# Tying nine kinds of instructions to written order in a two-layer hybrid decoder trunk, and moving attention's loads to earlier steps

## The chip, the cores and the metric

One Trainium2 chip, one of its cores. The metric is device time in microseconds (us) of one execution. The engines are named as in the profile: PE (matmul; PEld is its weight load), DVE (VectorE), ACT (ScalarE), POOL (GpSimd) and SP (SyncE, which here only issues DMAs). Each engine works through its own list of instructions in order and waits at an instruction until the semaphores that it needs have been raised.

## The reference

Two layers of a decoder trunk on 1024 tokens of width 1024, in float32. Each layer projects the normed input to eight head groups of width 256, four mLSTM heads (gates, a short convolution on q and k, a running-max stabiliser) and four retention heads (rotary q and k, fixed decay), and projects back:

```python
for l in range(DEPTH):
    ada = c_act @ w_ada[l] + b_ada[l]
    shift, scale, gate = jnp.split(ada, 3, axis=-1)
    h = rmsnorm(x, norm_g[l]) * (1.0 + scale[:, None, :]) + shift[:, None, :]
    p = h @ w_in[l]
    mq, mk, mv, mo, mz, mi, mf, rq, rk, rv, rz = split_cols(p)
    qk = jax.nn.silu(causal_dwconv(jnp.concatenate([mq, mk], axis=-1), conv_w[l], conv_b[l]))
    ...
    cell = mlstm_chunkwise(mq_c, mk_c, mv, mi + b_igate[l], mf + b_fgate[l])   # four heads
    y_m = jax.nn.sigmoid(mo) * head_layernorm(cell, gn_m[l], N_HEADS_MLSTM) * jax.nn.silu(mz)
    ret = retention_chunkwise(rotary(rq), rotary(rk), rv)                      # four heads
    y_r = head_layernorm(ret, gn_r[l], N_HEADS_RET) * jax.nn.silu(rz)
    y = jnp.concatenate([y_m, y_r], axis=-1) @ w_out[l]
    x = x + gate[:, None, :] * y
return rmsnorm(x, final_g)
```

## The kernel before

**Numbers.** Every float32 operand of a large product is kept as two float32r halves, a high half (a cast on ACT, `high`, L390) and the remainder (a subtraction on DVE or POOL, `low`, L395). A product is three matmuls, high by high, high by low and low by high (`mm3`, L164 to L166).

**Strassen pairs.** The projections are made in pairs of column blocks. A pair takes seven products instead of eight: `Feeder.quad` loads weight blocks, forms their sums (by an accumulating DMA from POOL's queue, L682, or by `total` on DVE, L686) and splits them; `build_forms` makes the matching sums of the normed input (L607 to L629, DVE); `pair_product` and `vpair_product` (for the values) run the seven products and add up their results out of PSUM (L743 to L755, L791 to L805).

**The order.** `jobs` lists the pairs of a layer (v: values of two heads, q and k, z: a gate pair, a: a z and an output gate column), and `slot_order` makes of them a list of slots, one product each. A slot of q, k, z or a is 12 matmuls of 512 columns, one of v 24 matmuls of 256. After each slot `tick()` advances all side work: generators that do a few instructions and then yield the number of ticks until their next turn. So everything has a place in a written order, given by the slot at which its generator resumes.

**Side work in that written order.**
- `gate_chain` (L485 to L571): cumulative sums of the gates, on DVE rows of 4 partitions, launched once per layer ahead of the last projection (four ticks) that stands before the first value pair; its DVE part begins after `yield 7`.
- `rotary_tables` (L426 to L462, first layer): DVE computes angles of the rotary tables and stores them; `load_rotary` (L941) loads them when pair q4 begins.
- `ada_rows` (L286 to L296): sums of w_ada rows on DVE, each behind a load.
- `conv_chain`, `rot_done`: convolution or rotation of q and k, then `spill` (L900) stores them to DRAM, `k_store` (L867) a transposed copy of k; `gate_o`, `z_gate`, `o_gate` and `vpair_product.store` store gates and values.
- `attention` (L955): one generator per head. It goes through `TABLE`, one entry per tick: q, k, t, v and d load queries, keys, transposed keys, values and decay rows of chunk j (four chunks of 256); Q, K, s and m split or finish them; S makes scores, V values, U the state update. `normalise` and `finish` (L1133 to L1171) follow the values.

**Who decides the issue order.** PE's instructions keep their written order (a manual schedule, L1403). For the other engines and for SP's and POOL's DMA queues a scheduler sets the order when the program is built: it goes forward with a model of the engines' times, and takes on each engine the earliest written instruction whose inputs are ready in that model. An instruction whose inputs seem ready soon thus moves ahead of ones written before it. Buffers come from rings: 12 "acc" tiles of 128x512 (`NACC`), 12 "R", 5 "wH"; "n", "nd", "zt" and "kc" have one buffer each, "q" and "dm" two.

Of the kernel before, what the change touches and what calls it, by code (L numbers as in the profile page):

```python
# [87 lines left out]
def tile_hybrid_trunk(ctx, tc, x, xt, c, positions, w_ada, b_ada, norm_g, w_in, w_blk, w_val, conv_w, conv_b,  # L88
# [40 lines left out]

    def f(ap):  # L130
        return ap.bitcast(F32)

    clock = [0]
    pending = []
# [151 lines left out]
    def ada_rows(l, c0, accs):  # L286
        acc = wt("acc", 512, NACC)
        accs.append(acc)
        for k in range(KT):
            raw = wt("acc", 512, NACC)  # L290
            Q.dma_start(raw, w_ada[l, k * P:(k + 1) * P, c0:c0 + 512])
            yield 2
            if k == 0:
                V.tensor_scalar(acc, raw, cact[:, 0:1], None, ALU.mult)
            else:
                V.scalar_tensor_tensor(acc, raw, cact[:, k:k + 1], acc, ALU.mult, ALU.add)  # L296

    def ada_columns_later(l):
        cl = cols[l][0]
# [124 lines left out]
    rdr = [[dpool.tile([P, HALF], F32, name=f"rdr{i}{j}") for i in range(2)] for j in range(2)]  # L424

    def rotary_tables():  # L426
        c1, c2, c3 = two_pi_split()
        ts = [wt("acc", 512, NACC) for _ in range(3)]
        ang, turn, tmp, rnd, a1, pos = (t[:, i * CH:(i + 1) * CH] for t in ts for i in range(2))
        a2 = ang  # L430
        for n in range(4):
            i, cs = n // 2, slice((n % 2) * CH, (n % 2 + 1) * CH)
            if n == 0:
                Q.dma_start(pos.bitcast(I32), positions[0:1, 0:CH].to_broadcast([P, CH]))
                yield 2
            V.tensor_copy(ang, pos.bitcast(I32))
            if n < 3:
                Q.dma_start(pos.bitcast(I32), positions[0:1, (n + 1) * CH:(n + 2) * CH].to_broadcast([P, CH]))
            V.tensor_scalar(ang, ang, kc[:, C_FREQ:C_FREQ + 1], None, ALU.mult)
            V.tensor_copy(a1.bitcast(F32R), ang)  # L440
            V.tensor_tensor(a2, ang, a1, ALU.subtract)
            V.tensor_scalar(turn, a1, c3, None, ALU.mult)
            V.scalar_tensor_tensor(turn, a2, c3, turn, ALU.mult, ALU.add)
            V.scalar_tensor_tensor(turn, a2, c2, turn, ALU.mult, ALU.add)
            yield 1
            for src, cc in ((a1, c2), (a2, c1), (a1, c1)):
                V.tensor_scalar(tmp, src, cc, None, ALU.mult)
                V.tensor_scalar(rnd, tmp, MAG_I, -MAG_I, ALU.add, ALU.add)
                V.tensor_tensor(tmp, tmp, rnd, ALU.subtract)
                V.tensor_tensor(turn, turn, tmp, ALU.add)  # L450
                yield 1
            parts = ((1, 0.0, tmp), (0, 0.25, a1))
            for which, sh, dst in parts:
                if sh:
                    V.tensor_scalar(turn, turn, sh, None, ALU.add)
                V.tensor_scalar(rnd, turn, MAG_I, -MAG_I, ALU.add, ALU.add)
                V.tensor_tensor(dst, turn, rnd, ALU.subtract)
                yield 1
                V.tensor_scalar(dst, dst, 0.49999994, -0.49999994, ALU.min, ALU.max)
            for which, sh, dst in parts:  # L460
                Q.dma_start(rdr[which][i][:, cs], dst)
            yield 1  # L462
# [20 lines left out]
            yield  # L483

    def gate_chain(l, pgs, gt):  # L485
        bg = cols[l][1]
        COL = wt("COL", 8 * 16, 1)
        C4 = COL.rearrange("p (t k h) -> p t k h", t=8, k=4)
# [89 lines left out]
    def gate_o(src, g, store, sign=1.0):  # L578
        th = wt("acc", 512, NACC)
        A.activation(th, src, AF.Tanh, scale=0.5 * sign)  # L580
        V.scalar_tensor_tensor(g, th, 1.0, g, ALU.add, ALU.mult)
        Q.dma_start(store, g)

    def z_evac(res, m):
        def evac(half, pz):
# [172 lines left out]
    def vpair_product(l, F, heads):  # L758
        banks, keeps = [{}, {}], [{}, {}]

        def store(part, i, half, src):
            vH, vL = (wt("acc", 512, NACC, F32R) for _ in range(2))
            A.activation(vH, src, AF.Copy, scale=-1.0 if i else 1.0)
            yield 1
            if i:
                V.scalar_tensor_tensor(vL, src, -1.0, f(vH), ALU.mult, ALU.subtract)
            else:
                V.tensor_tensor(vL, src, f(vH), ALU.subtract)  # L768
            yield 1
            dst = vdr[l][heads[i]][half * 2 + part].rearrange("(i t p) c -> i p t c", i=2, p=P)  # L770
            for o, v in zip(dst, (vH, vL)):
                Q.dma_start(o, f(v).rearrange("p (t c) -> p t c", t=2))

        def product(n, part, w):
            b, form = PRODUCT[n]
            bank, keep = banks[part], keeps[part]
            new = b not in bank
            if new:
                bank[b] = ps_x() if b == "X" else ps_z()
            for t in range(2):  # L780
                ts = slice((2 * part + t) * P, (2 * part + t + 1) * P)
                for k in range(4):
                    h = F[form][k]
                    mm3(bank[b][:, t * HD:(t + 1) * HD], (h[0][:, ts], h[1][:, ts]), w[k],
                        new and k == t == 0, k == 3 and t == 1, b != "Y")
            if n == "a12":
                return
            with tc.high_priority():
                if n == "a11":
                    c = wt("acc", 512, NACC)  # L790
                    A.copy(c, bank["X"])  # L791
                    V.tensor_tensor(bank["Y"], bank["Y"], c, ALU.add)
                    launch(store(part, 0, 0, bank["Y"]))
                    del bank["Y"]
                elif n in ("S1", "S2"):
                    keep[n] = wt("acc", 512, NACC)
                    A.copy(keep[n], bank[b])
                elif n == "S3":
                    V.tensor_tensor(keep["S1"], bank["X"], keep["S1"], ALU.add)
                    launch(store(part, 1, 1, keep["S1"]))  # L800
                elif n == "S4":
                    V.tensor_tensor(keep["S2"], bank["Z"], keep["S2"], ALU.add)
                    launch(store(part, 0, 1, keep["S2"]))
                else:
                    launch(store(part, 1, 0, bank["X"]))  # L805
        return product

    def z_gate(src, g, sign, store=None):
# [3 lines left out]
        V.scalar_tensor_tensor(g, th, 1.0, src, ALU.add, ALU.mult)  # L812
        if store is not None:
            yield 1
            Q.dma_start(store, g)

    def o_gate(src, g, store, sign, wait=0):
        th = wt("acc", 512, NACC)
# [1 line left out]
        yield 1 + wait  # L820
        V.scalar_tensor_tensor(g, th, 1.0, g, ALU.add, ALU.mult)
        yield 1
        Q.dma_start(store, g)

    def z_done(store):
        def done(m, half, src):
# [40 lines left out]
    def k_store(src, l, hg, m, half):  # L867
# [2 lines left out]
        a = n // P  # L870
        V.transpose(zt[:, 0:n].rearrange("p (b a c) -> p a b c", a=a, c=32),
                    src[:, 0:n].rearrange("p (a b c) -> p a b c", a=a, c=32))
        Q.dma_start(kdr[l][hg][half][m * P:(m + 1) * P, 0:n], zt[:, 0:n])

    def k_load(l, hg, j):
        half = j // 2
# [8 lines left out]
    def k_split(kr, hg, j, kt, gt):  # L885
# [4 lines left out]
        for tt in range(2):  # L890
# [3 lines left out]
                e = C_KS + 3 * h + (tt if j in WHOLE else 2)  # L894
                s = kc[:, e:e + 1]
            dH, dL = (x[:, tt, :].rearrange("p (b c) -> p b c", c=32) for x in kt[j])
            A.activation(dH, k3[:, tt], AF.Copy, scale=s)
            V.scalar_tensor_tensor(dL, k3[:, tt], s, f(dH), ALU.mult, ALU.subtract)

    def spill(src, l, hg, which, m, half):  # L900
        dst = (kfr if which else qdr)[l][hg][half].rearrange("(a p) t -> a p t", p=P)
        if which:
            k_store(src, l, hg, m, half)
        Q.dma_start(dst[m], src)

    def conv_done(l, hg, which):
        halos = [wt("halo", 3, 4) for _ in range(2)]
# [33 lines left out]
    def load_rotary(rot):  # L941
        for which in range(2):
            for i in range(2):
# [3 lines left out]
                rot[which].append(t[:, 0:HALF])  # L947

    busy = [False]
    TABLE = ("q0 k0 d0 t0", "", "v0", "Q0 K0 m0 d1", "s0 k1", "S0", "m1 q1 K1", "v1", "Q1", "V001", "S1 t1", "U01",  # L950
             "k2 q2 d2", "s1 v2", "V10 U2 m2 K2 Q2", "S2", "k3 d3", "V11 U3", "t2 q3 K3", "s2 v3", "", "V20 U4 m3 Q3",
             "S3", "", "V21 U5", "", "", "", "V30", "V31", "")
    RELEASE = 22

    def attention(l, hg, gt):  # L955
# [39 lines left out]
        def dm_make(j):  # L995
            if ml and j < NCH:
                dm = dms[j]
                for tt, (a, b) in enumerate(((0, 256), (256, 384)) if j in WHOLE else ((0, 128), (128, 256))):
                    G.affine_select(dm[:, a:b], dm[:, a:b], [[1, b - a]], ALU.is_ge, BIG, base=0, channel_multiplier=-1)
                    A.activation(dm[:, a:b], dm[:, a:b], AF.Exp, scale=-1.0, bias=gt["C4"][:, 2 * j + tt, 0, h:h + 1])  # L1000

        def piece(t, i, dt, a, n):
            o = i * 512 + dt * CH + a
# [129 lines left out]
        def normalise(j, tts, src):  # L1133
# [19 lines left out]
                G.tensor_tensor(rs, va, mhalf[:, 0:n], ALU.pow)  # L1153
            yield 1
            nmu = wt("nmu", 2, 2)[:, 0:n]
            V.scalar_tensor_tensor(nmu, mv3[:, a:b, 0], -1.0, rs, ALU.mult, ALU.mult)
            for i, tt in enumerate(tts):
                A.activation(nrm[j][:, tt, :], src[tt], AF.Identity, scale=rs[:, i:i + 1], bias=nmu[:, i:i + 1])
            if tts[-1] == 1:
                yield 1  # L1160
                yield from finish(j)
# [1 line left out]
        def finish(j):  # L1163
            half = j // 2
            z = wt("zt", 512, 1)
            V.transpose(z.rearrange("p (b t c) -> p t b c", b=8, c=32), nrm[j].rearrange("p a (b c) -> p a b c", c=32))
            yield 1
            for tb in range(4):
                src = z[tb * 32:(tb + 1) * 32, :].rearrange("p (b t) -> p b t", b=8)
                o = tb * P + (j % 2) * 64  # L1170
                Q.dma_start(ndr[l][hg][half][:, :, o:o + 64].rearrange("b j t -> j b t"), src)  # L1171

        krs = {}

# [514 lines left out]
```

## Time and profile before

| | us |
|---|---|
| median of 3 runs | 2354.99 (2350.48 to 2364.80) |
| the profiled execution | 2353.71 |
| its span, first to last instruction | 2352.0 |
| PE busy | 2150.1 (91%) |
| DVE busy | 1835.5 (78%) |
| ACT busy | 1146.7 (49%) |
| POOL busy | 950.8 (40%) |

The mean granted clock of PE is 0.966 of full speed. A profile line of a view that groups instructions names the line of the kernel, the engine, the operation, and the tiles as out<-in; a line of a wait says which instruction waited for which, the microseconds in total, how often, and the longest. In the timeline a line begins with the start and the duration in us, and ends, where the engine sat idle before it, with that idle time and what ended it.

### The profile page before, as it was taken

Reading aid. Unit: us, or ns where it says so; the run is one execution under the profiler, and the core shown is the slowest. Engines: PE = TensorE matmul, PEld = TensorE weight load, DVE = VectorE, ACT = ScalarE, POOL = GpSimd, SP = SyncE. Lnnn points to the kernel's source line nnn. Section 1 sums busy time; section 2 is a strip of 40 time slices with the busy share of each in tenths; the row PEclk is TensorE's granted clock in tenths of the full one; section 3 lists DMA queues with packets and bytes.
Section 4 is the critical chain, followed back from the end, with each engine's and each line's share of the span. In section 5 each row is a group of like instructions: output and inputs, shape, how many; then the busy total and the mean of one; then the engine's idle time right before and its main releaser. Section 6 shows DMA issues by size and latency. Waiting matters only on the chain. (4 is left out here: it accounts for less than half of the span.)

```text
span 2352.0 us, 35304 instructions
## 1 busy us (share of the span) xinstructions
PE 2150.1 (91%) x11483; PEld 1853.0 (79%) x11483; DVE 1835.5 (78%) x3301; ACT 1146.7 (49%) x2157; POOL 950.8 (40%) x842
## 2 busy tenths in 40 slices
PE   5969999989899989999997898998999899899998
PEld 4768788878787777788785787987988887777887
DVE  5898788888889899793538788787697878977753
ACT  5634344434555556553544333543555455555442
POOL 0342234443454444414366334544434343443223
PEclk8989999999999999999998899999999999999999
DMA  7237678887686667686632776876866676665974
GB/s 253 64 117 207 191 215 222 232 229 190 179 235 179 183 164 204 172 273 219 213 110 64 202 209 185 225 194 177 221 169 188 185 206 178 165 185 172 273 259 118
DMA packets 452550, 448.32 MB, mean 191 GB/s; under 512 B 191218, under 2 KB 309754, under 8 KB 452364
## 3 DMA queue, kind: packets, MB, share of 16 engines
q1 hardware_dynamic: 432636, 410.14, 56.6%
q0 software_dynamic: 19584, 35.66, 9.9%
q8 instruction: 90, 1.47, 0.3%
q14 instruction: 96, 0.79, 0.1%
q10 hardware_dynamic: 144, 0.26, 0.0%
HBM read 322.69 MB, written 123.24 MB: 190 GB/s over the span
## 5 line engine op out<-in xcount | busy, mean ns | idle before, releaser
L395 POOL TENSOR_TENSOR R<-R,wH 128x512 fp32r<-128x512 f32 x276 | 386.3, 1407 | 479.2 <-ACT wH L390 308.4
L390 ACT CAST wH<-R 128x512 fp32r<-128x512 f32 x616 | 376.3, 617 | 360.9 <-PE px L165 98.5
L164 PE MATMUL px<-b,wH 128*128 128x512 f32 x912 | 362.1, 397 | 11.9 <-DVE acc L749 6.0
L165 PE MATMUL px<-b,wH 128*128 128x512 f32 x912 | 359.8, 395 | 0.0
L166 PE MATMUL px<-b,R 128*128 128x512 f32 x912 | 359.1, 394 | 0.0
L395 DVE TENSOR_TENSOR R<-R,wH 128x512 fp32r<-128x512 f32 x340 | 264.7, 781 | 105.5 <-ACT wH L390 102.5
L165 PE MATMUL pz<-b,wH 128*128 128x512 f32 x704 | 279.2, 397 | 5.1 <-DVE b L1240 5.1
L164 PE MATMUL pz<-b,wH 128*128 128x512 f32 x704 | 279.8, 397 | 0.0
L166 PE MATMUL pz<-b,R 128*128 128x512 f32 x704 | 278.2, 395 | 0.0
L164 PEld LDWEIGHTS px<-b,wH 128*128 128x128 f32 x912 | 174.5, 191 | 50.1 <-ACT acc L743 8.6
L164 PE MATMUL px<-wH,b 128*128 128x256 f32 (+1 forms) x576 | 179.5, 312 | 28.6 <-ACT acc L791 15.5
L166 PEld LDWEIGHTS px<-b,R 128*128 128x128 f32 x912 | 173.7, 190 | 37.6
L165 PE MATMUL px<-R,b 128*128 128x256 f32 (+1 forms) x576 | 178.7, 310 | 24.3 <-DVE R L395 24.3
L165 PEld LDWEIGHTS px<-b,wH 128*128 128x128 f32 x912 | 174.2, 191 | 33.4
L166 PE MATMUL px<-wH,b 128*128 128x256 f32 (+1 forms) x576 | 177.7, 308 | 0.0
L682 POOL DMA_DIRECT2D R<-in_w_blk_dram x104 | 92.0, 885 | 209.0 <-DMA R<-in_w_blk_dram 96.4
L165 PEld LDWEIGHTS pz<-b,wH 128*128 128x128 f32 x704 | 134.9, 192 | 31.6 <-DVE b L1240 5.9
L166 PEld LDWEIGHTS pz<-b,R 128*128 128x128 f32 x704 | 134.8, 192 | 29.1
L164 PEld LDWEIGHTS pz<-b,wH 128*128 128x128 f32 x704 | 135.2, 192 | 26.4 <-DVE acc L752 0.3
L164 PE MATMUL pz<-wH,b 128*128 128x256 f32 (+1 forms) x448 | 137.1, 306 | 18.5 <-DVE acc L768 13.8
L164 PEld LDWEIGHTS px<-wH,b 128*128 128x128 f32 x576 | 118.5, 206 | 34.1 <-ACT acc L791 17.2
L844 POOL TENSOR_TENSOR q<-acc,q 128x512 fp32r<-128x512 f32 x64 | 91.7, 1432 | 122.8 <-ACT q L843 115.1
(370 smaller groups left out, 5433.8 us busy)
## 6 DMA issues: line engine op xcount, KB each, us to landing
R<-in_w_blk_dram SPq DMA_DIRECT2D x276, 256.0 KB
vdr<-acc SPq DMA_DIRECT2D x128, 256.0 KB
ring<-vdr SPq DMA_DIRECT2D x64, 512.0 KB
R<-in_w_out_dram SPq DMA_DIRECT2D x128, 256.0 KB
R<-in_w_blk_dram POOLq DMA_DIRECT2D x104, 256.0 KB, 4.6
R<-in_w_val_dram SPq DMA_DIRECT2D x80, 256.0 KB
gdr<-acc SPq DMA_DIRECT2D x64, 256.0 KB
acc<-in_w_ada_dram SPq DMA_DIRECT2D x64, 256.0 KB
```

What stands on the lines that cost most here:

```text
L164: PE.matmul(o, lt[0], rt[0], start=start, stop=False, skip_group_check=more)
L165: PE.matmul(o, lt[0], rt[1], start=False, stop=False, skip_group_check=more)
L166: PE.matmul(o, lt[1], rt[0], start=False, stop=stop, skip_group_check=more)
L390: A.copy(h, r)
L395: eng.tensor_tensor(lo, r, f(h), ALU.subtract)
L682: G.dma_start(raw[n], src, accum_op=ALU.add)
L844: eng.tensor_tensor(dst[1], src, f(dst[0]), ALU.subtract)
```

## The change

Two helpers are new. `late(ins)` pins an instruction: `keep_in_program_order` adds an edge, without a semaphore, from the instruction written just before it on the same engine, so that the scheduler may not issue it ahead of that one. Instructions written later may still go ahead of it. `Later` is a stand-in for the DVE engine that pins every instruction called through it. Pinned are the stores of gates, values, queries, keys and normed heads, the adaptive sums, the key splits, the making of the decay rows, the norms and their transpose, and all DVE instructions of the gate chain and the rotary tables. In attention's `TABLE` loads and splits change their steps; scores, values, updates, value loads and d loads keep theirs. Numbered from 0, the moves are: t1 from 10 to 9, k2 and q2 from 12 to 10, s1 from 13 to 12, K2 from 14 to 12, Q2 from 14 to 13, t2 from 18 to 16, k3 from 16 to 17, s2 from 19 to 18, K3 from 18 to 19, Q3 and m3 from 21 to 20.

```diff
+    def late(ins):
+        tc.keep_in_program_order(ins)
+        return ins
+
+    class Later:
+        def __getattr__(self, name):
+            call = getattr(nc.vector, name)
+            return lambda *a, **k: late(call(*a, **k))
...
-                V.tensor_scalar(acc, raw, cact[:, 0:1], None, ALU.mult)
+                late(V.tensor_scalar(acc, raw, cact[:, 0:1], None, ALU.mult))
             else:
-                V.scalar_tensor_tensor(acc, raw, cact[:, k:k + 1], acc, ALU.mult, ALU.add)
+                late(V.scalar_tensor_tensor(acc, raw, cact[:, k:k + 1], acc, ALU.mult, ALU.add))
...
     def rotary_tables():
+        V = Later()
...
     def gate_chain(l, pgs, gt):
+        V = Later()
...
-        Q.dma_start(store, g)
+        late(Q.dma_start(store, g))
...
-                Q.dma_start(o, f(v).rearrange("p (t c) -> p t c", t=2))
+                late(Q.dma_start(o, f(v).rearrange("p (t c) -> p t c", t=2)))
...
-        Q.dma_start(kdr[l][hg][half][m * P:(m + 1) * P, 0:n], zt[:, 0:n])
+        late(Q.dma_start(kdr[l][hg][half][m * P:(m + 1) * P, 0:n], zt[:, 0:n]))
...
-            A.activation(dH, k3[:, tt], AF.Copy, scale=s)
-            V.scalar_tensor_tensor(dL, k3[:, tt], s, f(dH), ALU.mult, ALU.subtract)
+            late(A.activation(dH, k3[:, tt], AF.Copy, scale=s))
+            late(V.scalar_tensor_tensor(dL, k3[:, tt], s, f(dH), ALU.mult, ALU.subtract))
...
-        Q.dma_start(dst[m], src)
+        late(Q.dma_start(dst[m], src))
...
-    TABLE = ("q0 k0 d0 t0", "", "v0", "Q0 K0 m0 d1", "s0 k1", "S0", "m1 q1 K1", "v1", "Q1", "V001", "S1 t1", "U01",
-             "k2 q2 d2", "s1 v2", "V10 U2 m2 K2 Q2", "S2", "k3 d3", "V11 U3", "t2 q3 K3", "s2 v3", "", "V20 U4 m3 Q3",
+    TABLE = ("q0 k0 d0 t0", "", "v0", "Q0 K0 m0 d1", "s0 k1", "S0", "m1 q1 K1", "v1", "Q1", "V001 t1", "S1 k2 q2", "U01",
+             "s1 d2 K2", "v2 Q2", "V10 U2 m2", "S2", "t2 d3", "V11 U3 k3", "s2 q3", "v3 K3", "Q3 m3", "V20 U4",
              "S3", "", "V21 U5", "", "", "", "V30", "V31", "")
...
-                    G.affine_select(dm[:, a:b], dm[:, a:b], [[1, b - a]], ALU.is_ge, BIG, base=0, channel_multiplier=-1)
-                    A.activation(dm[:, a:b], dm[:, a:b], AF.Exp, scale=-1.0, bias=gt["C4"][:, 2 * j + tt, 0, h:h + 1])
+                    late(G.affine_select(dm[:, a:b], dm[:, a:b], [[1, b - a]], ALU.is_ge, BIG, base=0, channel_multiplier=-1))
+                    late(A.activation(dm[:, a:b], dm[:, a:b], AF.Exp, scale=-1.0, bias=gt["C4"][:, 2 * j + tt, 0, h:h + 1]))
...
-            V.scalar_tensor_tensor(nmu, mv3[:, a:b, 0], -1.0, rs, ALU.mult, ALU.mult)
+            late(V.scalar_tensor_tensor(nmu, mv3[:, a:b, 0], -1.0, rs, ALU.mult, ALU.mult))
             for i, tt in enumerate(tts):
-                A.activation(nrm[j][:, tt, :], src[tt], AF.Identity, scale=rs[:, i:i + 1], bias=nmu[:, i:i + 1])
+                late(A.activation(nrm[j][:, tt, :], src[tt], AF.Identity, scale=rs[:, i:i + 1], bias=nmu[:, i:i + 1]))
...
-            V.transpose(z.rearrange("p (b t c) -> p t b c", b=8, c=32), nrm[j].rearrange("p a (b c) -> p a b c", c=32))
+            late(V.transpose(z.rearrange("p (b t c) -> p t b c", b=8, c=32), nrm[j].rearrange("p a (b c) -> p a b c", c=32)))
...
-                Q.dma_start(ndr[l][hg][half][:, :, o:o + 64].rearrange("b j t -> j b t"), src)
+                late(Q.dma_start(ndr[l][hg][half][:, :, o:o + 64].rearrange("b j t -> j b t"), src))
```

More of the change, by code (lines that the diff above doesn't have):

```diff
@@ L814, in z_gate @@
             yield 1
-            Q.dma_start(store, g)
+            late(Q.dma_start(store, g))
     def o_gate(src, g, store, sign, wait=0):
@@ L822, in o_gate @@
         yield 1
-        Q.dma_start(store, g)
+        late(Q.dma_start(store, g))
     def z_done(store):
```

## The prediction

> **What bounds the kernel now.** I read the page's head, then the stretches of the span, then who PE (the matmul engine) waits for, and last the order of instructions around single waits.
>
> ```profile
> span 2352.0 us, 35304 instructions
> PE 2150.1 (91%) x11483; PEld 1853.0 (79%) x11483; DVE 1835.5 (78%) x3301; ACT 1146.7 (49%) x2157; POOL 950.8 (40%) x842
> ```
>
> The span lies within an execution of 2353.7 us, 1.3 us under the shown median of 2355.0; the sum is made against the 2353.7. PE is busy for 91% and its order is fixed by hand, so time can only come out of PE's idle 202 us and of what such idling entails. In the stretches (length, then busy time of PE, PEld, DVE, ACT, POOL, then the granted clock):
>
> ```profile
> core 0: us, PE busy (x) PEld busy (x) DVE busy (x) ACT busy (x) POOL busy (x), PEclk, DMA share, GB/s
> 105.00:185.00 80.00, 54.26 (x379) 52.84 (x378) 74.12 (x107) 25.79 (x44) 34.45 (x22) 0.87 0.43 121
> 185.00:250.00 65.00, 60.60 (x406) 55.93 (x404) 53.12 (x121) 29.57 (x50) 19.72 (x16) 0.97 0.67 190
> 250.00:1000.00 750.00, 699.88 (x3777) 605.60 (x3778) 646.05 (x1197) 376.38 (x740) 326.07 (x305) 0.97 0.72 200
> 1260.00:1330.00 70.00, 46.47 (x298) 44.28 (x297) 63.95 (x72) 25.97 (x44) 38.57 (x24) 0.80 0.38 108
> 1330.00:2100.00 770.00, 720.97 (x4045) 632.35 (x4044) 629.18 (x1166) 384.23 (x750) 330.97 (x311) 0.98 0.70 194
> ```
>
> Two kinds of stretch matter. At the first value products of each layer (105 to 250, 1260 to 1330) DVE is the bound: it is busy 74.12 of 80 us while PE manages 54.26. In the long stretches with attention PE is nearly full and loses 750 - 699.88 = 50.1 and 770 - 720.97 = 49.0 us in many small waits. PE waits for:
>
> ```profile
> PE px L165 <- DVE R L395: 24.3, 5, 7.2
> PE pa L1092 <- ACT sH L1048: 15.6, 5, 5.0
> PE pz L164 <- DVE acc L768: 13.8, 3, 7.9
> PE pa L166 <- DVE b L898: 13.4, 7, 4.5
> PE pa L166 <- POOL sL L1049: 10.6, 7, 2.6
> PE pa L1010 <- POOL q L844: 7.5, 5, 3.9
> ```
>
> (total, times, longest). The first and third are the value products; the others belong to attention: score halves (L1048, L1049), key splits (L898), query splits (L844).
>
> A wait costs more than itself. After one of 2.49 us the granted clock was 0.50 over the next 3.4 us:
>
> ```profile
> 354.13 0.38 PE L166 MATMUL pa<-ring,sL 128*128 128x256 f32 x1 [2.49 <-POOL sL L1049]
> 355.00:358.40 3.40, 3.40 (x10) 2.73 (x10) 3.17 (x7) 0.11 (x1) 2.63 (x3) 0.50 0.79 151
> ```
>
> So I add length times (1 - PEclk) to the idle time. Value stretches: idle 25.7 + 4.4 + 23.5 and clock 10.4 + 2.0 + 14.0, together 80.0 us. Attention stretches: idle 99.2 and clock 22.5 + 15.4, together 137.1; per us of wait 137.1 / 99.2 = 1.38 us are lost.
>
> [...]
>
> **The change, part by part.** It adds no work and takes none away. A pinned instruction can't be issued ahead of the one written just before it on its engine; others may still pass it. The second part moves steps in attention's table.
>
> *Gate sums and rotary tables (DVE).* In the written order the gate chain's DVE part begins 8 ticks after its launch, four of them value slots. In the trace it runs far earlier:
>
> ```profile
> 104.33 1.77 DVE L513 TENSOR_TENSOR q<-q,nd 4x512 f32<-4x512 f32 x1
> 106.02 1.20 DVE L516 TENSOR_TENSOR_SCAN dm<-ones,nd 4x512 f32<-4x512 f32 x1
> ...
> 108.94 2.28 DVE L517 TENSOR_TENSOR_SCAN n<-ones,q 4x512 f32<-4x512 f32 x1
> 111.15 0.39 DVE L512 TENSOR_SCALAR cf<-q 4x512 f32<-4x512 f32 x1
> ...
> 113.97 1.40 DVE L521 TENSOR_SCALAR q<-kc 4x512 f32<-4x512 f32 x1
> 115.40 1.64 DVE L581 SCALAR_TENSOR_TENSOR acc<-acc,acc 128x512 f32<-128x512 f32 x1
> 116.97 0.67 DVE L513 TENSOR_TENSOR q<-q,cf 4x512 f32<-4x512 f32 x1
> 117.57 1.27 DVE L516 TENSOR_TENSOR_SCAN dm<-ones,dm,cf 4x512 f32<-4x512 f32 x1
> ...
> 119.35 0.67 DVE L395 TENSOR_TENSOR R<-R,wH 128x512 fp32r<-128x512 f32 x1
> 120.08 0.58 PE L165 MATMUL px<-R,b 128*128 128x256 f32 x1 [5.15 <-DVE R L395]
> 117.07 11.60 SPq L582 DMA_DIRECT2D gdr<-acc  x2
> ```
>
> Of the 15.0 us before the low half L395, seven shown gate instructions take 1.77 + 1.20 + 2.28 + 0.39 + 1.40 + 0.67 + 1.27 = 8.98. Behind them L395 comes 5.15 us late for PE, and the gate store L582 waits for L581 in SP's queue, with later weight loads behind it (11.60 us for the two stores). Nobody needs the gates before the first mLSTM head, whose first decay row is made at 553 us:
>
> ```profile
> L999 POOL TENSOR_SCALAR_AFFINE_SELECT dm<-dm x64: 282/399/978, 553.4 to 2114.7; 128x128 f32<-128x128 f32 x48, 128x256 f32<-128x256 f32 x16
> ```
>
>  Pinned, the gate sums stand behind the form sums and lows written before them. But their DVE time remains to be done, and while DVE is the bound, order alone wins only what DVE idles: 5.88 + 11.88 + 6.05 = 23.8 us over the three stretches. Upper end: the chain slides wholly into the attention stretch, where DVE idles 750 - 646.05 = 104 us, and 70% of the 80.0 us comes back: 56. Lower end: a loss of 10, if the rotary tables are held up. Their cover is this:
>
> ```profile
> 240.21 0.38 SPq L945 DMA_DIRECT2D b<-rdr  x1
> 268.22 0.69 DVE L929 TENSOR_TENSOR acc<-acc,b 128x512 f32<-128x512 f32 x1
> ```
>
> The last table is fetched 28.0 us ahead of the first rotation; PE arriving 18 us sooner leaves 10, and if the pinned tables slip by more, the rotations hold the PSUM banks and PE waits. I take three quarters of 23.8: **-18 us**, nearest to the DVE-bound rows.
>
> *Decay rows, adaptive sums, key splits, norms.* These now run when written and not when their inputs seem ready. What the early issue costs on in-order engines:
>
> ```profile
> ACT q L843 <- DMA acc<-qdr: 70.1, 28, 4.2
> POOL dm L999 <- DMA dm<-mdr: 66.1, 30, 8.0
> ACT dm L1000 <- POOL dm L999: 60.5, 39, 8.4
> DVE acc L296 <- DMA acc<-in_w_ada_dram: 32.5, 22, 4.1
> ACT b L897 <- DMA acc<-kdr: 29.5, 21, 3.7
> 797.38 0.40 ACT L1000 ACTIVATE dm<-dm,COL 128x128 f32<-128x128 f32 x1 [1.42 <-POOL dm L999]
> 798.07 0.40 ACT L1000 ACTIVATE dm<-dm,COL 128x128 f32<-128x128 f32 x1 [0.29 <-POOL dm L999]
> 798.38 0.49 ACT L1048 CAST sH<-acc 128x384 fp32r<-128x384 f32 x1
> ```
>
> At 797 ACT stands in front of the score half that PE waits for, 1.42 + 0.29 us for decay rows wanted by a later chunk. Pinned, the decay pair comes at steps m0 to m3 of the table, when its load is long in; behind a waiting pinned L1000 stand then the same highs and score halves as now.
>
> *The table.* k2 and q2 load two steps earlier and split two and one earlier (K2 at 12, Q2 at 13, used by S2 at 15); t1, s1 one earlier, t2 two, s2 one; Q3 and m3 one; k3, K3 one later. Per head that moves on SP two loads of 256 KB and eight of 64 KB forward, past the weight loads and stores of the one or two products between, and t2 past d3 and k3 as well. A load wants a buffer and waits for no engine's result but the spill, done steps before; the weight loads that it passes are put back by its own issue, a third of a us or so each (the L945 row above took 0.38), which I cost at nothing since these loads run eight products ahead of their use. POOL's queue gets nothing new. Splits get one or two steps more before their use: the key splits of U2 and U4 go from 1 and 2 steps ahead to 2 and 3. A step is at least one product, 12 matmuls.
>
> Of attention's waits I credit all of L898 (13.4) and half of L1048, L1049 and L844 (33.7 / 2 = 16.9): 30.3 x 1.38 = 41.8, and half of that again, since PE set free runs into the next late operand: **-21 us**. Ends: nothing, and all of 47.1 x 1.38 = 65.
>
> *Stores, and new waits.* A pinned store no longer passes loads written before it, which serves the loads; the store itself and the buffer it frees come later. Behind a store that waits stand the weight loads (L385), and behind those the splits and PE; pinning doesn't shorten the wait for the data, so today's waits of that kind stay:
>
> ```profile
> SPq L904 <- DVE acc L863: 118.7, 35, 9.8
> ACT acc L763 <- DMA ndr<-zt: 3.0, 1, 3.0
> ```
>
> The second row is the nearest for an engine that waits for a store. The norms (L1158) and their transpose, pinned, release their single buffers later. Price: nothing, up to one wait of 15.6 / 5 = 3.1 us in each of 16 heads, 16 x 3.1 x 1.38 = 68. I take four heads with a wait of 13.4 / 7 = 1.9 us, because the cover (two steps between norm and the next values) is thin only where PE has caught up: 4 x 1.9 x 1.38 = **+10.5 us**.
>
> Sum: -18 - 21 + 10.5 = -28.5; 2353.7 - 28.5 = 2325.2, and 1.3 more against the shown median: **2326 us**, 1.2% less.
>
> [...]
>
> **The rivals.**
>
> *Buffers and norms decide: slower.* All stores, norms and transposes are held back while k2 and q2 take two of the 12 acc buffers two steps earlier; evacuations wait for a buffer, PSUM banks stay full, PE waits once per head. For it: the L763 row, and 35 waits on L904. Against it: that row is one wait in the whole run. Place: each of the 16 heads; price 68 us: -39 + 68 = +29, 2353.7 + 29 = 2383. It decides from 39 / (16 x 1.38) = 1.8 us of new wait per head.
>
> *The waits only move: no difference.* The pins name one predecessor, and where that one ran early too, nothing is held; and DVE stays at 78%. Then -6 (a quarter of 23.8) - 12 + 10.5 = -7.5, 2346. For it: 74.12 of 80 us on DVE. Against it: L1000 ahead of L1048 is order, not load.
>
> *The gate chain leaves the value stretch altogether.* -56 - 21 + 10.5 = -66.5, 2287. For it: DVE's 104 idle us later; against it: it is written within that stretch.
>
> **How the numbers follow.** Chances: forecast 0.48 (own range 2300 to 2345), the larger gain 0.14, moved waits 0.17, buffers 0.21. About 1% (23 us) is what a measurement of this kernel can tell from no change. A sixth of the forecast's case (0.08) falls within it, with all of the moved waits: same 0.25; faster 0.40 + 0.14 = 0.54; slower 0.21. The range runs from the larger gain's time to that of the buffers, 2287 to 2384: half of each lies outside, 0.07 and 0.10.
>
> **What would show it.** Right: L395's wait on PE falls from 24.3 to under 12 and no gate-chain line stands ahead of the first lows; PEclk of the two value stretches rises above 0.90; L1000 waits for L999 under 20 us in all; L898 vanishes from PE's waits. Wrong: PE's idle total stays near 202 us; new PE waits on acc evacuations (L743, L763, L791) or on L1158; rotary multiplies (L929) waiting for L945. If DVE in 105 to 185 is still above 90% and PE no fuller, the first term has failed.

## The result, and the profile after

The changed kernel takes 2286.1 us (median of 4 runs, 2280.25 to 2286.23), the kernel before 2359.9 (4 runs, 2350.48 to 2366.07): ratio 0.9685, 95% interval 0.9643 to 0.9726. That is 3.15% less, 74 us, where 28.5 were forecast, and 1 us below the lower end of the range. The direction was right; the forecast gain was well under half of the measured one. The two profiled executions lie 67.5 us apart (2353.71 and 2286.23); what is worked out from traces below goes by them.

The two helpers move the lines: L390, L395 and L743 of before are L399, L404 and L754; L898, L1000, L1048 and L1049 are L909, L1011, L1059 and L1060; L1156 and L1158 are L1167 and L1169. The page's head after:

```profile
span 2284.5 us, 35248 instructions
PE 2134.0 (93%) x11483; PEld 1840.7 (81%) x11483; DVE 1827.6 (80%) x3301; ACT 1150.6 (50%) x2157; POOL 957.2 (42%) x842
```

PE's idle time fell from 201.9 to 150.5 us, by 51.4, and the span by 67.5: each us of wait that went took 67.5 / 51.4 = 1.31 us with it. The forecast's factor was 1.38. The stretches after (length, busy time of PE, PEld, DVE, ACT, POOL, granted clock):

```profile
105.00:185.00 80.00, 62.36 (x467) 60.65 (x466) 77.63 (x121) 28.15 (x53) 36.36 (x25) 0.89 0.48 132
185.00:250.00 65.00, 56.91 (x340) 49.81 (x339) 54.36 (x117) 25.25 (x43) 17.59 (x15) 0.95 0.73 203
250.00:1000.00 750.00, 711.59 (x3882) 617.47 (x3881) 660.36 (x1231) 392.24 (x763) 331.62 (x308) 0.98 0.73 207
1260.00:1330.00 70.00, 56.93 (x322) 51.11 (x321) 66.00 (x94) 27.12 (x47) 26.77 (x19) 0.88 0.65 182
1330.00:2100.00 770.00, 741.01 (x4181) 650.88 (x4180) 647.69 (x1228) 408.84 (x795) 350.12 (x323) 0.98 0.72 199
```

PE's idle time fell from 25.7 to 17.6 and from 23.5 to 13.1 in the DVE-bound stretches, and from 50.1 to 38.4 and from 49.0 to 29.0 in the long ones; from 185 to 250 it rose from 4.4 to 8.1. PE waits after, among others (total, times, longest):

```profile
PE pz L173 <- DVE acc L779: 16.0, 3, 7.6
PE pa L175 <- DVE b L909: 15.3, 7, 5.3
PE px L173 <- ACT acc L754: 8.2, 3, 5.2
PE pa L1103 <- ACT sH L1059: 8.0, 3, 3.7
PE pa L173 <- ACT nd L1116: 7.6, 4, 4.0
PE pa L1103 <- POOL sL L1060: 5.7, 6, 2.4
PE px L173 <- ACT acc L802: 5.6, 5, 2.3
PE px L174 <- DVE R L404: 4.2, 3, 2.0
```

The wait for the lows (24.3 before) is nearly gone. All rows of the score halves together fell from 32.9 to 15.3 us, the query splits (7.5 before) are gone from the view, and the key splits hold PE as long as before (13.4). A row of before that the prediction's list leaves out fell as well. It is an evacuation (a copy of results out of PSUM) in the value pairs, L802 after:

```profile
PE px L164 <- ACT acc L791: 15.5, 7, 3.8
```

PE runs the same matmuls in the same order in both kernels, so the starts of the n-th matmul can be compared. Worked out from the two traces:

```
matmul    before us   after us   ahead by   gained since the row above
   600       166.1      151.0      15.2      +15.1   value products, layer 1
  1200       268.9      260.7       8.2       -7.0
  6000      1248.0     1223.9      24.1      +15.9   attention, layer 1
  6600      1379.9     1347.1      32.8       +8.7   value products, layer 2
 10800      2188.7     2121.6      67.1      +34.3   attention, layer 2
```

The value stretches (up to matmul 1200, and 6000 to 6600) give 8.2 + 8.7 = 16.9 us, where 18 were forecast. The other 50.2 come from the attention and projections between them, for which the forecast had -21 + 10.5, so 10.5 us. Both rows of the clearest stretch, before and then after:

```profile
1400.00:1730.00 330.00, 313.67 (x1894) 281.30 (x1893) 262.72 (x472) 155.25 (x310) 152.50 (x139) 0.98 0.73 200
```

```profile
1400.00:1730.00 330.00, 328.15 (x2007) 294.62 (x2006) 273.69 (x523) 173.10 (x340) 157.25 (x145) 1.00 0.77 213
```

After the change PE is busy for 328.15 of 330 us there. PE's waits in this stretch, before:

```profile
PE px L164 <- ACT acc L791: 7.9, 3, 3.8
PE pa L1101 <- DVE cL L1074: 3.2, 1, 3.2
PE pa L166 <- POOL sL L1049: 2.4, 2, 1.8
```

and all that the view lists after:

```profile
PE px L173 <- ACT acc L802: 1.5, 3, 0.7
PE px L173 <- DVE acc L867: 0.3, 1, 0.3
```

The place at 797 us that the prediction shows (ACT idle in front of decay rows, with a score half behind them) reads after:

```profile
772.29 0.68 ACT L1011 ACTIVATE dm<-dm,COL 128x128 f32<-128x128 f32 x2
...
776.85 0.52 ACT L1059 CAST sH<-acc 128x384 fp32r<-128x384 f32 x1 [0.69 <-DVE acc L1040]
```

The decay rows run without a wait (60.5 us over the run before, none after), and the score half waits only for its own input. Not only they changed. ACT's waits for the running sums and the norms, before and then after:

```profile
ACT cH L1072 <- DVE cf L1069: 96.5, 35, 9.2
ACT n L1158 <- DVE nmu L1156: 76.8, 36, 5.4
```

```profile
ACT cH L1083 <- DVE cf L1080: 43.9, 27, 4.8
ACT n L1169 <- DVE nmu L1167: 36.3, 21, 3.7
```

### The profile page after: what moved, and what is told of

The parts are those of the page before. It is cut to its first block, busy times and chain, and to the rows that moved or that the text cites. A ratio compares the mean times of both kernels' runs of the same rounds, so it can differ in the third digit from the quotient of the medians.

```text
span 2284.5 us, 35248 instructions
## 1 busy us (share of the span) xinstructions
PE 2134.0 (93%) x11483; PEld 1840.7 (81%) x11483; DVE 1827.6 (80%) x3301; ACT 1150.6 (50%) x2157; POOL 957.2 (42%) x842
## 5 line engine op out<-in xcount | busy, mean ns | idle before, releaser
L399 ACT CAST wH<-R 128x512 fp32r<-128x512 f32 x616 | 378.2, 618 | 463.7 <-PE px L174 122.1
L404 POOL TENSOR_TENSOR R<-R,wH 128x512 fp32r<-128x512 f32 x276 | 395.9, 1441 | 508.1 <-ACT wH L399 344.2
L404 DVE TENSOR_TENSOR R<-R,wH 128x512 fp32r<-128x512 f32 x340 | 258.4, 764 | 112.3 <-ACT wH L399 107.5
L174 PE MATMUL pz<-b,wH 128*128 128x512 f32 x704 | 276.2, 392 | 5.1 <-DVE b L1251 5.1
L173 PE MATMUL pz<-b,wH 128*128 128x512 f32 x704 | 276.6, 393 | 1.9 <-DVE acc L763 1.8
L175 PEld LDWEIGHTS px<-b,R 128*128 128x128 f32 x912 | 175.6, 193 | 38.4
L173 PE MATMUL px<-wH,b 128*128 128x256 f32 (+1 forms) x576 | 176.3, 306 | 18.3 <-DVE acc L867 6.3
L175 PE MATMUL px<-wH,b 128*128 128x256 f32 (+1 forms) x576 | 174.2, 302 | 0.0
L173 PE MATMUL pz<-wH,b 128*128 128x256 f32 (+1 forms) x448 | 135.8, 303 | 17.3 <-DVE acc L779 16.0
L175 PE MATMUL pz<-wH,b 128*128 128x256 f32 (+1 forms) x448 | 135.2, 302 | 0.7 <-DVE b L1251 0.7
L174 PE MATMUL pz<-R,b 128*128 128x256 f32 (+1 forms) x448 | 135.1, 302 | 0.0
```

What stands on the lines that cost most here:

```text
L173: PE.matmul(o, lt[0], rt[0], start=start, stop=False, skip_group_check=more)
L174: PE.matmul(o, lt[0], rt[1], start=False, stop=False, skip_group_check=more)
L175: PE.matmul(o, lt[1], rt[0], start=False, stop=stop, skip_group_check=more)
L399: A.copy(h, r)
L404: eng.tensor_tensor(lo, r, f(h), ALU.subtract)
```

## The experiments

In the reports below a ratio is to the kernel before on the same chip, with its 95% interval. Line numbers of single variants differ by up to two from those of the changed kernel. "Matmul 1200" and the like are starts compared as above.

**The table alone, the pins alone, and the value stretches' pins alone.** The first has only the new TABLE, the second all pins with the old one, the third only these:

```diff
     def rotary_tables():
+        V = Later()
...
     def gate_chain(l, pgs, gt):
+        V = Later()
```

> The new table alone, nothing pinned. Theory A (most of the gain in the attention stretches is order on ACT, DVE and SP, so it comes from the pins): 2335 to 2360, less than a third of the gain of some 72 us. Theory B (the earlier loads and splits bring the attention part, some 50 us): 2295 to 2315. Theory C (pins and table only work together, since an unpinned split runs early anyway): 2345 to 2375.

> All pins, the old table. Theory A: 2290 to 2310, most of the gain. Theory B: 2335 to 2350, only the value stretches' 16 us. Theory C: above 2340, since pinned splits then come too late for the updates that need them (waits of PE on the key splits L898 grow above 20 us).

> Only the gate chain and the rotary tables are pinned, old table. All theories: the two value stretches win some 16 us net, 2336 to 2344; the attention stretches stay as before. If the gain is above 30 us, the gate chain also ruled what came after it.

Measured: table 0.9956 (0.9939 to 0.9973); pins 0.9988 (0.9968 to 1.0009); gate and rotary pins 0.9969 (0.9945 to 0.9992). None does what the whole does, and the first two together are 0.9944 if they multiply. The third gains 16.1 us by matmul 600, and in its trace almost all of it is given back by the end (0.8). Most of that goes between matmul 1200 and 6000, where PE idles 65.9 us instead of 56.1: PE that comes sooner does run into other waits there. By the ratio 0.31%, some 7 us, are left, so how much is given back isn't certain. The pinned gate chain also makes PE wait where the kernel before has no such wait, for a matmul of the chain itself. In the third kernel, and then in the changed one:

```profile
PE pa L554 <- DVE cL L140: 14.0, 2, 8.1
```

```profile
PE pa L554 <- DVE cL L140: 4.0, 1, 4.0
```

With the pins alone PE waits for the key splits:

```profile
PE pa L175 <- DVE b L909: 42.8, 18, 4.6
PE pa L173 <- ACT b L908: 30.3, 9, 6.7
```

With the old table the pinned key splits stand too close to the state updates that need them: 73.1 us of PE's waits, where before had 13.4 for L898. That is what theory C expected of this kernel.

**The whole without the value stretches' pins**, the two lines above taken out of the changed kernel:

> All other pins and the new table, gate chain and rotary tables free. If the parts add up: 2300 to 2308 (the change's time and 16 us), the waits of the first value products on the low halves back near 24 us. If it falls to 2290 or less, the value stretches give back later what they win.

Measured: 2288.7 us, 0.9693 (0.9671 to 0.9714). Nearly the whole gain is there without them, and the time is in the range of the second case (what the value stretches win is given back later). In this trace matmul 600 gains 0.9 and matmul 1200 5.8 us, and the wait for the lows is back at 25.6 us.

**The key splits.** First all pins but theirs, with the old table; then the changed kernel without their pins:

```diff
-            late(A.activation(dH, k3[:, tt], AF.Copy, scale=s))
-            late(V.scalar_tensor_tensor(dL, k3[:, tt], s, f(dH), ALU.mult, ALU.subtract))
+            A.activation(dH, k3[:, tt], AF.Copy, scale=s)
+            V.scalar_tensor_tensor(dL, k3[:, tt], s, f(dH), ALU.mult, ALU.subtract)
```

> Old table, all pins except that of the key splits. Theory C1 (with the old table the pinned key split stands too late for its state update, and that alone eats what the other pins win): 2295 to 2320, PE's waits on the key split lines fall from 73 us to under 20. Theory C2 (pins and loads need each other all over the table): above 2335, with other waits of attention in their place.

> New table, all pins except that of the key splits. C1: the pin itself wins little, 2280 to 2300. If the pin is needed as well (a free key split floats in front of more urgent work on ACT and DVE): 2310 or more.

Measured: 0.9725 (0.9702 to 0.9747) and 0.9722 (0.9700 to 0.9744). Both times are in the range of theory C1, and PE's waits for the key splits in the first are 11.3 us. So with the key splits free the old table does as well as the new one, and the other pins carry 2.8% without the table. Then all pins with half of the table's moves each: t1 to 9, t2 to 16, s1 to 12, s2 to 18 in the first, all the others in the second.

```diff
-..., "V001", "S1 t1", "U01", "k2 q2 d2", "s1 v2", ..., "k3 d3", "V11 U3", "t2 q3 K3", "s2 v3", ...
+..., "V001 t1", "S1", "U01", "s1 k2 q2 d2", "v2", ..., "t2 k3 d3", "V11 U3", "s2 q3 K3", "v3", ...
```

> All pins, and of the table only the moves of the transposed keys: t1, s1, t2, s2. C1: nearly the whole gain, 2285 to 2305, key split waits under 20 us. C2: above 2320.

> All pins, and of the table only the moves of k2, q2, k3, K2, Q2, K3, Q3, m3; the transposed keys as before. C1: still near the old time, 2335 to 2360, key split waits above 50 us. C2: 2310 to 2330, half of the gain.

Measured: 0.9691 (0.9661 to 0.9721) and 0.9881 (0.9848 to 0.9914). PE's wait for the key splits in the first:

```profile
PE pa L175 <- DVE b L909: 7.2, 4, 3.6
```

and in the second:

```profile
PE pa L175 <- DVE b L909: 36.0, 17, 4.1
PE pa L173 <- ACT b L908: 28.0, 10, 7.8
```

Four entries of the table, each one or two steps earlier, are what the pinned key splits need. They turn 0.9988 into 0.9691. The second kernel, between its two expectations, still has 64.0 us of waits for the key splits and yet gains 1.2%: the other moves help too while the key splits come late, but beside the four they add nothing that can be told from no change (0.9685 with all moves).

**One group of pins at a time**, old table, each of this kind:

```diff
-        Q.dma_start(dst[m], src)
+        late(Q.dma_start(dst[m], src))
```

> Old table, only the stores are pinned. The pins but for the key split win some 64 us with the old table; gate chain and rotary have some 7 to 15 of that. Theory D1 (SP's queue: a store issued early and waiting for its data holds up the loads behind it): 2315 to 2330, the largest part. Theory D2 (the parts on ACT, DVE and POOL win): 2350 to 2362. Theory D3 (a shuffled order, each part alone within noise): all four of these kernels within 1% of before.

> Old table, only the decay rows are pinned. D2: the 60 us that ACT waits on POOL's L999 vanish and PE's waits on the score halves L1048 and L1049 (31 us) halve: 2330 to 2345. D1: 2350 to 2362.

> Old table, only the norms (factor, scaling, transpose) are pinned. D2: ACT's waits on the factor (L1158 for L1156, 103 us for both tiles) halve and some 15 us are won: 2335 to 2350. D1: 2350 to 2365.

> Old table, only the adaptive sums are pinned. D2: DVE's waits of 37 us on w_ada loads vanish, some 5 to 15 us won: 2345 to 2355. D1: 2350 to 2362.

Measured: stores 0.9906 (0.9878 to 0.9933); decay rows 1.0027 (1.0011 to 1.0043); norms 0.9921 (0.9892 to 0.9950); adaptive sums 1.0005 (0.9986 to 1.0023). So none of the theories holds for all four: stores win less than D1 said, norms are where D2 put them, decay rows and adaptive sums win nothing. All four lie within 1% of before, as D3 said, but stores and norms are clear of no change. In the trace with the decay rows pinned ACT's wait for L999 is gone, as D2 expected, but PE's waits for the score halves are 31.8 us, where before had 32.9. With the norms pinned ACT's waits for the factor fall from 102.7 to 56.8 us. The profiled execution of this third kernel lies 14 us above its median, so its trace isn't read for the gain. SP's waits at the stores of queries and keys (L904, L915 after) and of the transposed keys (L873, L884 after), in the kernel before and then in the changed one:

```profile
SPq L904 <- DVE acc L863: 118.7, 35, 9.8
SPq L904 <- DVE acc L931: 114.4, 35, 11.5
...
SPq L873 <- DVE acc L871: 31.7, 25, 3.2
```

```profile
SPq L884 <- DVE acc L882: 129.6, 31, 13.3
SPq L915 <- DVE acc L942: 61.9, 18, 11.6
...
SPq L915 <- DVE acc L874: 32.9, 17, 7.8
```

Summed over all rows that these views list, the waits at the stores of queries and keys fell from 369.9 to 140.0 us, and those at the store of the transposed keys, written ahead of it, rose from 59.9 to 169.5: together 429.8 became 309.5. With the stores alone pinned the sum is 379.9.

**Stores and norms together, and the whole without them.** Both pinned with all else as before; then the changed kernel without the one, without the other, with neither; and one with only stores, norms and key splits pinned and the new table:

> The kernel before with only the stores and the norms (with their transpose) pinned, table as before. Parts add up: stores alone gave 0.9906 and norms alone 0.9921, so about 0.983, 2315 to 2325 us. Parts help each other (a store kept in its place is worth more when the norm that feeds it is in its place, since both stand in the same chain from values to normed heads): 0.977 or less, 2305 us or less. Parts take the same waits away: 0.988 or more, 2332 us or more.

> The changed kernel without the pins on the stores; all other pins and the new table stay. Parts add up: it loses the 22 us that stores won alone, about 0.978, 2308 us. Parts help each other: 0.985 or more, 2320 us or more. Others take the same waits away: within 10 us of the changed kernel, 0.973 or less.

> The changed kernel without the pins on the norms and their transpose. Parts add up: it loses 18 us, about 0.976, 2304 us. Parts help each other: 0.984 or more, 2318 us or more. Others take the same waits away: within 8 us of the changed kernel, 0.972 or less.

> The changed kernel with neither stores nor norms pinned; the other pins and the new table stay. If the two stand in for each other: 0.985 or more, 2320 us or more, since together they win 35 us alone. If the remaining pins with the new table take the same waits away: 0.972 to 0.978, 2290 to 2305 us.

> Only stores, norms and key splits pinned, with the new table; the adaptive sums, decay rows, gate sums and rotary tables are free as before. If those four do nothing in the whole either: 0.966 to 0.972, 2278 to 2294 us, no slower than the changed kernel. If the decay rows' place ahead of the score halves matters in the whole (ACT waits 60 us for them before, none after): 0.975 or more, 2300 us or more.

Measured: together 0.9852 (0.9823 to 0.9882), so they add up (0.9906 x 0.9921 = 0.9828). Taken out of the whole each costs little: 0.9720 (0.9689 to 0.9750) without stores, 0.9720 (0.9684 to 0.9757) without norms, against 0.9685 (0.9643 to 0.9726). That is what "others take the same waits away" said, though these intervals overlap that of the whole, so the cost of one group may be nothing. With neither, 0.9783 (0.9755 to 0.9811), 2304.6 us, at the upper edge of the second expectation: both together cost 1.0%, clear of the whole's interval. The last kernel is at 0.9743 (0.9709 to 0.9776), 2293.7 us, at the upper edge of its first expectation: adaptive sums, decay rows, gate sums and rotary tables are worth about 0.6% in the whole, and the intervals of the two overlap a little, so this isn't settled.

**The rotary tables.** The changed kernel with their line `V = Later()` taken out:

> The changed kernel with the rotary tables' DVE instructions free again; the gate sums stay pinned. If the pinned tables hold the buffers that the evacuation at 240 us needs: that wait of 5.2 us goes, the gain over the kernel before at matmul 1200 is 13 us or more (changed kernel: 8.2), and the whole takes 2278 to 2284 us, 0.964 to 0.967. If the give-back has another cause (the gate sums themselves, which still have to be done): gain at matmul 1200 stays at 6 to 10 us and the whole at 0.968 to 0.972.

Measured: 2280.7 us (2277.41 to 2283.68), 0.9679 (0.9651 to 0.9707). In the changed kernel the timeline of ACT and that of SP's queue at the end of the first value stretch read:

```profile
243.00 0.33 SPq L471 DMA_DIRECT2D rdr<-acc  x1
...
244.78 0.59 ACT L754 COPY acc<-px 128x512 f32<-128x512 f32 x1 [3.56 <-DMA rdr<-acc]
```

with the tables free:

```profile
237.59 0.33 SPq L470 DMA_DIRECT2D rdr<-acc  x1
...
239.36 0.59 ACT L753 COPY acc<-px 128x512 f32<-128x512 f32 x1 [1.43 <-PE pz L175]
```

Pinned, the table's last two stores come 5.4 us later, and an evacuation of PSUM waits for the acc buffer that the store frees; PE stands behind it for 5.2 us. Free, the lead at matmul 1200 is 13.3 us instead of 8.2, and at the end 75.4 instead of 67.1. The rotary pins don't do this alone. All seven kernels of this document that pin the rotary tables and the stores have this wait, 5.2 to 5.5 us, and the three that pin the tables and leave the stores free have at most 1.2 us there, with a lead of 12.2 to 14.6 us at matmul 1200 instead of 8.2 to 11.3. The mechanism is shown by the traces, and the wait, the lead and the time in us are those of the first expectation. As a time the changed kernel and the one with free tables aren't told apart: their intervals overlap widely.

## Why the prediction was wrong in size

**What bounds, and the factor: right.** PE's waits were the place, and 1.31 us per us of wait is near the 1.38.

**The value stretches (-18): right in the stretch.** 16.9 us were gained there, L404's wait is 4.2 (forecast under 12), DVE is still at 77.63 of 80 us while PE rose from 54.26 to 62.36. The clock rose to 0.89 and 0.88, not above 0.90. The term's reason, DVE's idle time, holds over the whole of the two stretches: up to matmul 1200 (from 105 us) and from 6000 to 6600 DVE idled 22.8 + 18.0 us before and 16.9 + 4.9 after, 19.0 less. It doesn't hold for the first gain. From the matmul that starts at 105 us to matmul 600 DVE idled only 0.5 us before, and PE gained 14.9 us there because 14.7 us of DVE's work moved behind that point; about half was given back by matmul 1200. The time of 2287 that the rival "the gate chain leaves the value stretch" gave was met by chance: the chain's own matmuls (L554) start at 172 us, still inside the stretch, DVE is as full there as before, and that rival had the forecast's -21 and +10.5 for the attention, where 50.2 us were gained. The lower end's cause was real too, by another way: not rotations that wait for a table, but an evacuation that waits for a table's buffer. But the first term isn't what the two pins are worth. Without them these stretches still gain 5.8 + 5.4 = 11.2 us in the trace (matmuls 1 to 1200 and 6000 to 6600), and the whole is at 0.9693. Without the rotary pin alone they gain 13.3 + 8.8 = 22.1. The term also had no price for the wait of the chain's own matmul (4.0 us).

**Stores and norms (+10.5): wrong in sign, the step that failed first.** I took these pins as a later release of buffers, and the rows of early issue for decay rows and key splits alone. The same pattern stood in the profile for the norms: 76.8 us in which ACT stood before L1158 waiting for L1156, more than the 60.5 that I used for decay rows. Alone the stores win 0.94% and the norms 0.79%, together 1.48%, 35 us of 2357, and taken out of the whole both cost 1.0%. By the traces, each a single execution, this term is where most of the miss lies. The changed kernel without these pins gains 50.1 us, 12.2 + 6.7 of them in the value stretches, so 31.2 outside them; the changed kernel gains 50.2 there. The pins thus bring 19.0 us where 10.5 were charged, a miss of 29.5 out of the 38.6 between the 28.5 forecast and the 67.1 gained. The waits that I priced do occur: PE waits 7.6 us in four places (1.3 before) for L1116, which writes the single buffer "nd" that the norm's transpose frees, close to the 4 x 1.9 us assumed. In the two long ones, of 4.0 and 3.2 us, L1116 starts within 0.2 us of the end of that transpose. But with the norms unpinned they are still 6.9 us, so the pins don't make them. How the stores' order in SP's queue reaches PE wasn't followed wait by wait: which loads come sooner by it stays open.

**Decay rows: the wait was right, its worth wrong.** 60.5 us of ACT's waiting went to nothing, as forecast under 20, and alone that makes the kernel no faster (1.0027) and leaves PE's waits for the score halves where they were (31.8 us for 32.9). The rows of 797 us are one case in which the wait lay on PE's path, and I took it for the rule.

**Key splits and table (all of L898): wrong as a mechanism.** The wait didn't vanish (15.3). Pinning makes it 73.1, the four moves of t and s bring it back. I credited the pin and the moves as if both helped; the four moves repair what the pin does, and with the key splits free the table changes nothing (0.9725 and 0.9722).

**The halvings of the second term: too strong.** I credited half of the score and query waits and halved the sum again, since PE set free would run into the next late operand. That fits one pin at a time: the gate and rotary pins alone lose most of their 16 us again, and decay rows alone gain nothing. It fails for the whole: from 1400 to 1730 us almost nothing was left to run into. Leaving one group free costs 0.35% where alone it won 0.8 to 0.9%; that would fit a set of waits that several pins each can remove, but it isn't shown, since 0.35% isn't clear of noise. In size the term is off by about 10 us: the 31.2 us above that the changed kernel gains outside the value stretches without the pins on stores and norms, against 21. In the whole change PE's waits fell elsewhere than the sum said: those for score halves and query splits by 25.1 us of 40.4, those for the key splits not at all, and those for the evacuation L791, which the sum left out, by 9.9 of 15.5.

Why the whole is more than its parts is shown only so far: the singles (stores, norms, decay rows, adaptive sums, gate and rotary pins, table) sum to -2.2%, the key splits' pin was not run alone, the whole is -3.15%, and free key splits with all other pins give -2.8% with either table. Which waits make up the rest of about 1% isn't settled.

## What to carry to other kernels

A scheduler that takes whatever seems ready can put waits at the head of in-order engines and queues (before, 60.5 us of ACT's at the decay rows and 118.7 in SP's queue in one row of the store L904); look for them in every engine's list of waits, the norms' and stores' too, and not only where one row shows PE suffering. Edits of order need not add up: a pin can uncover a step that was written too late, so pin and step have to be tried together, and single trials of the parts say little of the whole. A wait that a pin removes is not yet time: the 60.5 us of the decay rows went, and no time with them. A pinned chain that holds shared buffers can hold up others; here that shows in the traces (5.2 us of PE's waiting) and not in the time.

## What the runs showed of the hardware

In the kernel before, the length of a wait on PE alone doesn't tell what it costs in clock: after 3.22 us that ended at 1633.3 the granted clock was 1.00 over the next 3.4 us, after 2.10 us that ended at 1894.5 it was 0.50:

```profile
1633.34 0.50 PE L1101 MATMUL pa<-cL,q 128*128 128x256 f32 x2 [3.22 <-DVE cL L1074]
1894.50 0.80 PE L1092 MATMUL pa<-ring,sL 128*128 128x258 f32 x2 [2.10 <-POOL sL L1049]
```

```profile
1633.40:1636.80 3.40, 3.40 (x28) 3.40 (x29) 1.69 (x3) 0.98 (x3) 1.28 (x3) 1.00 0.67 208
1894.40:1897.80 3.40, 3.30 (x15) 3.30 (x16) 3.00 (x10) 1.75 (x5) 1.00 (x3) 0.50 1.06 377
```

What decides between the two wasn't shown. In the changed kernel, from 1400 to 1730 us, the longest of PE's waits was 0.7 us and the mean granted clock 1.00.
